# An encoder block's instruction planner: its estimates of matmul times, transfer latencies and transfer rate are set anew

## Chip, cores and metric

The kernel runs on one core of a Trainium2 chip. The metric is the device time of one execution in microseconds. Before the change it is 3083.7 us, the median of three runs (3083.41 to 3086.44).

## What is computed

One layer of an encoder for 1024 tokens of 1024 numbers, all in float32:

```python
h  = rmsnorm(x, norm1_w)
p  = h @ w_in                      # q, k, v of attention; q, k, v, z of the delta rule; decay, beta; two gates
oa = rmsnorm(softmax(q1 k1) v - lam * softmax(q2 k2) v, subln_w) * 0.8    # 8 heads
og = rmsnorm(gated_delta_rule(forward) + gated_delta_rule(backward), gdn_norm_w) * silu(z)   # 8 heads
x  = x + (sigmoid(gate_a) * (oa @ w_proj_attn) + sigmoid(gate_g) * (og @ w_proj_gdn)) @ w_out
h2 = rmsnorm(x, norm2_w)
# 16 experts; each takes the 128 tokens with the highest softmax(h2 @ w_router)
x  = x + sum_e scatter(top_e * ((silu(h2_e @ w_gate_e) * (h2_e @ w_up_e)) @ w_down_e))
out = rmsnorm(x, norm_f_w)
```

The delta rule works in chunks: in each, a triangular system is solved, and a state of 128 x 128 numbers is carried from one chunk to the next, in both directions.

## The kernel before

**Stages.** The first norm and the decay (to about 44 us); the delta rule, head after head (to 960); attention (to 1617); the two projections, the output projection with the second norm and the router, and the choice of tokens, called top-k (to about 1910); then 16 experts, and a last norm of all rows.

**How products are made.** A float32 product is made of three products of float32r parts: a high part (a rounded copy, by ScalarE) and a low part (the rest, a subtraction by VectorE or GpSimd). That pair of instructions is called a split. `mm3` issues the three matmuls, with 512 columns for dense work. Dense products read weights that are loaded in tiles of 512 KB, split and then used (class `Dense`); those of the delta rule's and attention's input, and of the gates, are the filler for TensorE while heads and rows go through dependent steps.

**Delta rule, by head** (class `Head`). `decay` loads two rows of `dG` from DRAM, each broadcast to 128 partitions, and `main` makes `U2` from them. The diagonal blocks are written to DRAM (`dl`), read back in another order as `Lu`, solved by VectorE in 15 steps, written to DRAM again (`dw`) and read back as `WN`. Three `merges` tasks then join blocks: a block transpose on VectorE (`flip`), a matmul, a copy, a matmul, a predicated copy. Two `chain` tasks carry the states of both directions; every step is a matmul that waits for VectorE or ScalarE.

**Experts** (class `Experts`). An expert has 4 units. A unit takes four parts of 1 MB of gate and up weights and two of down weights; SP loads a part into one of ten buffers, the splitter turns it into one of four pairs of high and low parts (ScalarE copies 128 x 2048 numbers, VectorE subtracts), and `worker` uses it for 12 matmuls of 512 columns. `gate` makes the activation of a unit, `prep` transposes it on TensorE (four transposes), copies the result out of PSUM (ScalarE, 128 x 512) and makes its low part, which the down product needs. The buffer of a part is free when VectorE has subtracted. At the end `tail` reads all rows back, `final_pair` applies the last norm to two tiles of them, and `last` adds what the last expert gives and scatters its rows.

**What sets the order.** No order is written down. Tasks hand their instructions to `Emit`, which holds an imagined clock for each engine and one for transfers. `run` takes, among the instructions whose inputs are issued, the one that could start first by these clocks, and by priority where two could start at once; `issue` moves the clock of the engine on by the cost that the helper (`mm`, `act`, `tt`, `dma`) gave. Each engine of the chip then works through its own instructions in just that order and waits, at each, for what it needs. The clocks are in ns. `LAT` has what passes between one engine's end and another's start; a transfer ends 650 after SP has issued it plus its length divided by a rate, and one after another.

Of the kernel before, what the change touches and what calls it, by code (L numbers as in the profile page):

```python
# [45 lines left out]
# ---------------------------------------------------------------- emission order  # L46
#
# Everything on the chip's SBUF and PSUM lies in two tiles; tags name slots in them. The work
# is cut into tasks (generators); the instructions of a task go into its queue, and run() hands
# them on one by one, in the order in which an estimate of the engines' clocks lets them start.  # L50
# [25 lines left out]
class Block:  # L76
    """A range of SBUF (or all of PSUM): one tile at a time, each of one type."""
# [27 lines left out]
class Op:  # L105
    __slots__ = ("eng", "cost", "load", "acc", "fn", "block", "ready", "prio", "kind", "dma")


class Emit:
# [15 lines left out]
    # ---- slots  # L125
# [80 lines left out]
    # ---- tasks  # L206
# [66 lines left out]
    def op(self, eng, cost, fn, writes, reads, load=0, kind="", dma=0):  # L273
        o = Op()
        o.eng, o.cost, o.fn, o.load, o.kind, o.dma = eng, cost, fn, load, kind, dma
        o.acc = [self.region(a, True) for a in writes] + [self.region(a, False) for a in reads]
        o.prio = self.cur.opprio
        q = self.cur.q
        o.block = {p for p in q if p.eng and ((eng == "pe" and p.eng == "pe") or self.conflict(p, o))}
        o.ready = None if o.block else self.when(o)  # L280
        q.append(o)

    def order(self, a, ea, b, eb):
        """Whether b must wait for a: in PSUM also for other engines' accesses to its bank."""
# [14 lines left out]
    def issue(self, t, o):  # L299
# [4 lines left out]
        if o.dma:  # L304
            who = "dma"
            end = self.dma_clk = max(end + 650, self.dma_clk) + o.dma
# [73 lines left out]
    # ---- instructions  # L380

    def mm(self, out, lhsT, rhs, start, stop):
        n = free(rhs)
        if rhs.dtype == F32R:
            c, l = (n if n >= 256 else 4 * n) / 2.4 + 2.5, 55
        else:
            c, l = max(4 * n / 2.4 + 4, 214), 109
# [54 lines left out]
    def flip(self, out, in_):  # L442
        """Every 32 x 32 block transposed in its place."""
# [19 lines left out]
    def dma(self, out, in_):  # L463
# [3 lines left out]
        self.op("sp", 478, lambda: self.nc.sync.dma_start(out, in_), [out], [in_], 0, "dma", max(n / 360.0, 112))  # L467

    def pdma(self, out, in_):
# [3 lines left out]
        self.op("pool", 1100, lambda: self.nc.gpsimd.dma_start(out, in_), [out], [in_], 0, "pdma", max(n / 360.0, 112))  # L473
# [26 lines left out]
    def prsqrt(self, y, x, t):  # L500
        """The same with the steps on GpSimd."""
# [10 lines left out]
    def rsqrt(self, y, x, t):  # L512
        """y = x^-1/2 with t as room for two tiles."""
# [14 lines left out]
# ---------------------------------------------------------------- where things lie  # L528

def plan(e):  # L530
    """Blocks, and the tags in them: name, size, number, by phase."""
# [21 lines left out]
    # first norm, decay  # L553
# [3 lines left out]
    # gated delta rule  # L557
# [6 lines left out]
    # attention  # L564
# [4 lines left out]
    # projections  # L569
# [11 lines left out]
    # experts  # L581
# [10 lines left out]
    # psum  # L592
# [9 lines left out]
# ---------------------------------------------------------------- dense products  # L602

class Dense:
    """Products with streamed weights: a loader, a splitter into two float32r parts and the
    matrix work, which fills the tensor engine whenever nothing else can run."""
# [69 lines left out]
def proj_ns(g, evac, wait=None):  # L676
    """[n, s] product of one 128-column weight tile with the first norm's output."""
# [22 lines left out]
# ---------------------------------------------------------------- first norm  # L700
# [52 lines left out]
# ---------------------------------------------------------------- decay and beta  # L753

def logit_job(g):
    """Decay and beta logits [32, s]."""
# [83 lines left out]
# ---------------------------------------------------------------- gated delta rule  # L840
# [6 lines left out]
class Head:  # L847
# [66 lines left out]
    def decay(self, dr):  # L914
# [5 lines left out]
        e.dma(d.v.rearrange("p t x -> p (t x)"), bcast(g.dG[dr * 8 + h:dr * 8 + h + 1, :], [P, S]))  # L920
# [1145 lines left out]
```

## Time and profile before

| what | value |
|---|---|
| median of three runs | 3083.7 us |
| the profiled execution, span from its first to its last instruction | 3079.2 us |
| TensorE busy, share of the span | 2883.4 us, 94% |
| VectorE | 2361.6 us, 77% |
| ScalarE | 1750.1 us, 57% |
| GpSimd | 545.7 us, 18% |
| moved by DMA | 598.52 MB |

The page gives no other time of the profiled execution than its span; the runs' median lies 4.5 us above it. Busy shares are means over stages that differ: the same engine can be the limit in one and wait in another, so a stage is read from the busy time in its own stretch, and a wait from the instruction that waited and from what stood before it in its queue. Since every engine keeps to its order, a short instruction that waits holds up all that stands behind it, needed or not.

### The profile page before, as it was taken

The page shows a single profiled execution, that of the slowest core. Times are in us where ns is not written, and L with a number is a line of the kernel's source. Part 1 is how long each engine was busy: PE and PEld are TensorE (multiplying, and loading weights), DVE is VectorE, ACT ScalarE, POOL GpSimd, SP SyncE. Part 2 cuts the span into 40 slices and gives each one's busy share as a digit, 9 for nine tenths or more (in the row PEclk, how much of TensorE's full clock was granted, in tenths as well). Part 3 has the DMA queues.
Part 4 walks back from the last instruction along what each step waited for, and adds up shares of the span by engine and source line. Part 5 has one row for each costly group of instructions (what it writes and reads, how often), then busy time and mean ns, then how long its engine had stood idle before and what let it go on. Part 6 is the DMA issues. An engine that isn't in the chain of part 4 may idle for free.

```text
span 3079.2 us, 40415 instructions
## 1 busy us (share of the span) xinstructions
PE 2883.4 (94%) x14692; PEld 2378.0 (77%) x14692; DVE 2361.6 (77%) x3837; ACT 1750.1 (57%) x2669; POOL 545.7 (18%) x457
## 2 busy tenths in 40 slices
PE   7999999999998999999999993999999999999996
PEld 6787888778787878888787772888777777777775
DVE  7768778777865777777862466998888888888887
ACT  5435444444533666676752322777767767776775
POOL 3222312222222111111225334000000000000001
PEclk9999999999999999999999996999999999999998
DMA  4222322221232111112549635999999999999996
GB/s 137 55 73 72 83 71 58 79 70 55 80 80 57 42 49 49 49 49 58 175 141 290 206 110 233 364 372 382 361 367 364 365 368 371 366 367 366 364 335 246
DMA packets 203352, 598.52 MB, mean 194 GB/s; under 512 B 84224, under 2 KB 102016, under 8 KB 154000
## 3 DMA queue, kind: packets, MB, share of 16 engines
q1 hardware_dynamic: 189568, 561.86, 50.8%
q0 software_dynamic: 13584, 34.08, 4.0%
q8 instruction: 115, 1.88, 0.2%
q14 instruction: 85, 0.70, 0.1%
HBM read 534.99 MB, written 52.49 MB: 191 GB/s over the span
## 4 chain that ended last, share of the span: by engine, by line
PE 66%; DVE 18%; ACT 4%; DMA 4%; issue 3%; SPq 1%; POOL 1%; ACTq 0%; POOLq 0%; DVEq 0%
PE psum L388 62%; DVE B L406 6%; PE psum L392 4%; DVE B L431 4%; ACT B L400 2%; DVE B L435 2%; DVE A L406 1%; SPq L467 1%; ACT A L400 1%; DVE B L425 1%; ACT psum L400 1%; DVE C L457 1%; DVE C L458 1%; DMA B<-in_w_gu_dram 1%; DMA dw<-B 1%
## 5 line engine op out<-in xcount | busy, mean ns | idle before, releaser
L388 PE MATMUL psum<-A,W 128*128 128x512 f32 (+1 forms) x5856 | 1561.2, 406 | 22.9 <-DVE A L406 14.1
L388 PEld LDWEIGHTS psum<-A,W 128*128 128x128 f32 (+1 forms) x5856 | 1062.6, 188 | 244.7 <-DVE A L406 22.0
L388 PE MATMUL psum<-B 128*128 128x128 f32 (+3 forms) x3494 | 655.6, 324 | 14.3 <-DVE B L439 7.6
L388 PEld LDWEIGHTS psum<-B 128*128 128x128 f32 x3494 | 542.4, 190 | 93.1 <-DVE B L439 11.1
L400 ACT ACTIVATE B<-psum 128x512 f32<-128x512 f32 (+4 forms) x612 | 266.2, 441 | 409.2 <-PE psum L392 230.4
L400 ACT ACTIVATE B<-B 128x2048 fp32r<-128x2048 f32 (+5 forms) x339 | 378.2, 1124 | 175.1 <-DVE B L431 80.1
L410 POOL TENSOR_TENSOR W<-W,W 128x1024 fp32r<-128x1024 f32 (+1 forms) x105 | 264.1, 2516 | 954.8 <-ACT W L400 812.8
L406 DVE TENSOR_TENSOR B<-B,B 128x2048 fp32r<-128x2048 f32 (+2 forms) x187 | 367.1, 1971 | 31.8 <-ACT B L400 25.7
L388 PE MATMUL psum<-B,W 128*128 128x512 f32 x1536 | 375.6, 397 | 1.5
L388 PEld LDWEIGHTS psum<-B,W 128*128 128x128 f32 x1536 | 285.9, 188 | 77.0 <-DVE B L406 9.9
L400 ACT ACTIVATE B<-psum,B 128x128 f32<-128x128 f32 (+2 forms) x264 | 190.9, 728 | 197.3 <-PE psum L388 124.7
L392 PE MATMUL psum<-C,B 128*128 128x128 f32 (+1 forms) x1392 | 218.4, 280 | 76.2 <-DVE B L431 27.2
L406 DVE TENSOR_TENSOR A<-B,A 128x2048 fp32r<-128x2048 f32 x115 | 261.2, 2286 | 17.7 <-ACT A L400 16.4
L388 PE MATMUL psum<-A,B 128*128 128x512 f32 x1024 | 268.6, 401 | 6.1 <-DVE A L406 3.2
L392 PEld LDWEIGHTS psum<-C,B 128*128 128x128 f32 (+1 forms) x1392 | 170.1, 143 | 128.1 <-DVE B L431 35.1
L400 ACT ACTIVATE A<-B 128x2048 fp32r<-128x2048 f32 (+1 forms) x124 | 228.6, 1858 | 44.3 <-PE psum L388 32.4
L388 PEld LDWEIGHTS psum<-A,B 128*128 128x128 f32 x1024 | 190.8, 190 | 45.2 <-DVE A L406 3.9
L388 PE MATMUL psum<-B,B 128*128 128x128 f32 (+1 forms) x1024 | 211.2, 293 | 12.2 <-DVE B L444 10.1
L481 POOL DMA_INDIRECT dx<-B,C x15 | 23.9, 1591 | 1037.5 <-ACT B L400 1037.5
L388 PEld LDWEIGHTS psum<-B,B 128*128 128x128 f32 x1024 | 174.9, 191 | 40.3 <-DVE B L444 13.9
L435 DVE TENSOR_REDUCE B<-psum 128x1 f32<-128x1024 f32 (+1 forms) x136 | 157.2, 1157 | 54.1 <-PE psum L388 52.9
L410 POOL TENSOR_TENSOR B<-B,B 128x128 f32<-128x128 f32 (+3 forms) x98 | 129.9, 1329 | 307.4 <-ACT B L400 218.8
(95 smaller groups left out, 2786.2 us busy)
## 6 DMA issues: line engine op xcount, KB each, us to landing
B<-in_w_gu_dram SPq DMA_DIRECT2D x152, 1024.0 KB, 7.1
A<-in_w_gu_dram SPq DMA_DIRECT2D x78, 1024.0 KB, 7.3
B<-in_w_dn_dram SPq DMA_DIRECT2D x77, 1024.0 KB, 6.5
A<-in_w_dn_dram SPq DMA_DIRECT2D x37, 1024.0 KB, 6.3
W<-in_w_gu_dram SPq DMA_DIRECT2D x26, 1024.0 KB, 7.2
W<-in_w_gdn_dram SPq DMA_DIRECT2D x32, 512.0 KB, 3.7
B<-dG SPq DMA_DIRECT2D x32, 512.0 KB, 5.3
W<-in_w_proj_dram SPq DMA_DIRECT2D x32, 512.0 KB, 4.5
```

What stands on the lines that cost most here:

```text
L388: self.op("pe", c, lambda: self.nc.tensor.matmul(out, lhsT, rhs, start=start, stop=stop), [out], [lhsT, rhs], l, "mm")
L392: self.op("pe", 109, lambda: self.nc.tensor.transpose(out, in_, ident), [out], [in_, ident], 55, "tr")
L400: self.op("act", c, lambda: self.nc.scalar.activation(out, in_, func, **kw), [out] + w, [in_] + r, 0, "act")
L406: self.op("dve", 69 + 1.041 * free(out), lambda: self.nc.vector.tensor_tensor(out, a, b, op), [out], [a, b], 0, "tt")
L410: self.op("pool", 150 + 2.104 * free(out), lambda: self.nc.gpsimd.tensor_tensor(out, a, b, op), [out], [a, b], 0, "ptt")
L425: lambda: (self.nc.vector.tensor_scalar(out, a, s1, None, op0=op0) if s2 is None else self.nc.vector.tensor_scalar(out, a, s1, s2, op0=op0 ...
L431: lambda: self.nc.vector.scalar_tensor_tensor(out, a, s, b, op0=op0, op1=op1),
L435: self.op("dve", 69 + 1.041 * free(in_), lambda: self.nc.vector.tensor_reduce(out, in_, axis=AX.X, op=op), [out], [in_], 0, "red")
L457: (lambda: V.match_replace(y, val, x, -1.0), [y], [val, x], "mr"),
L458: (lambda: V.max_index(idx, val, x), [idx], [val, x], "maxi")]
L467: self.op("sp", 478, lambda: self.nc.sync.dma_start(out, in_), [out], [in_], 0, "dma", max(n / 360.0, 112))
L481: self.op("pool", 1100, lambda: self.nc.gpsimd.indirect_dma_start(out=dst, out_offset=bass.IndirectOffsetOnAxis(ap=idx, axis=0), in_=y, in ...
```

## The change

In `mm`, a float32r product of n columns is reckoned at (n + 43) / 2.4 ns in place of n / 2.4 + 2.5 (below 256 columns 4n / 2.4, without the 2.5), a float32 product at 4n / 2.4 + 9, at least 222, in place of 4n / 2.4 + 4, at least 214. The rate of transfers is 380 bytes per ns in place of 360. A transfer may carry an extra latency, `slow`, which delays what reads it, but not the transfers behind it; seven calls give one. Section comments and docstrings are blanked, so line numbers move by one or two. The computation is the same.

```diff
@@ issue
             who = "dma"
-            end = self.dma_clk = max(end + 650, self.dma_clk) + o.dma
+            end = max(end + 650, self.dma_clk) + o.dma
+            self.dma_clk = end - o.slow
@@ mm
         if rhs.dtype == F32R:
-            c, l = (n if n >= 256 else 4 * n) / 2.4 + 2.5, 55
+            c, l = (n + 43 if n >= 256 else 4 * n) / 2.4, 55
         else:
-            c, l = max(4 * n / 2.4 + 4, 214), 109
+            c, l = max(4 * n / 2.4 + 9, 222), 109
@@ dma (pdma has the same rate)
-    def dma(self, out, in_):
+    def dma(self, out, in_, slow=0):
-        self.op("sp", 478, lambda: self.nc.sync.dma_start(out, in_), [out], [in_], 0, "dma", max(n / 360.0, 112))
+        self.op("sp", 478, lambda: self.nc.sync.dma_start(out, in_), [out], [in_], 0, "dma", max(n / 380.0, 112) + slow, slow)
@@ Head.decay (and qG in Head.kvprep): broadcasts of dG
-        e.dma(d.v.rearrange("p t x -> p (t x)"), bcast(g.dG[dr * 8 + h:dr * 8 + h + 1, :], [P, S]))
+        e.dma(d.v.rearrange("p t x -> p (t x)"), bcast(g.dG[dr * 8 + h:dr * 8 + h + 1, :], [P, S]), 1700)
@@ Head.main: blocks read back, solution written (both halves)
-            e.dma(Lu[64 * dr:64 * dr + 64], dl[:, :, dr, :].rearrange("r q x -> q r x"))
+            e.dma(Lu[64 * dr:64 * dr + 64], dl[:, :, dr, :].rearrange("r q x -> q r x"), 800)
-        e.dma(dw[:, :, 1, :].rearrange("r q x -> q r x"), W[0:64])
+        e.dma(dw[:, :, 1, :].rearrange("r q x -> q r x"), W[0:64], 500)
@@ proj_job: gates and the other branch's part
-        e.dma(th.v, g.dgate[1 - k, n, :, hs])
+        e.dma(th.v, g.dgate[1 - k, n, :, hs], 1100)
-            e.dma(yv.v, g.dyg[sh, n])
+            e.dma(yv.v, g.dyg[sh, n], 1100)
```

What this does to the order is shown at three places. A row is one instruction or several equal ones; L388 and L389 are the matmul of `mm`, L392 and L393 the transpose, L400 and L401 `act`.

The first is TensorE in the middle of the experts, before. `psum<-C_76,B_82` are the transposes of an activation, the 128x512 rows are products of one unit's weights, 12 to a part (`B_7778`, `A_78` and `W_111` are the blocks of memory that they read).

```order
L388 MATMUL psum<-B_7778,W_111 128x512 x24
L388 MATMUL psum<-A_78,B_7778 128x512 x17
L392 MATMUL psum<-C_76,B_82 128x128 x4
L388 MATMUL psum<-A_78,B_7778 128x512 x7
L388 MATMUL psum<-B_7778,W_111 128x512 x24
L388 MATMUL psum<-A_78,W_111 128x512 x24
L388 MATMUL psum<-B_7778 128x512 x9
L392 MATMUL psum<-C_76,B_82 128x128 x4
L388 MATMUL psum<-B_7778 128x512 x15
L388 MATMUL psum<-A_78,W_111 128x512 x24
```

And now, the same work (`B_7815` and `W_112` are the same blocks).

```order
L389 MATMUL psum<-B_7815,W_112 128x512 x24
L389 MATMUL psum<-A_78,W_112 128x512 x24
L389 MATMUL psum<-B_7815 128x512 x23
L393 MATMUL psum<-C_76,B_82 128x128 x4
L389 MATMUL psum<-B_7815 128x512
L389 MATMUL psum<-A_78,W_112 128x512 x24
L389 MATMUL psum<-B_7815,W_112 128x512 x24
L389 MATMUL psum<-A_78,B_7815 128x512 x23
L393 MATMUL psum<-C_76,B_82 128x128 x4
L389 MATMUL psum<-A_78,B_7815 128x512
```

Before, the transposes stand 17 and 9 products into a group of 24; now 23 products in, one before its end, in all units but those that also hold the transposes of the next expert's rows.

The second is ScalarE at the end of the kernel, before. `B_82<-psum` is a unit's activation function, `B_7778<-psum` the copy of its transposes, 128x2048 a split's copy, 128x1024 the last norm.

```order
L400 ACTIVATE B_82<-psum 128x512
L400 ACTIVATE B_7778,C_77<-B_13903 128x1024
L400 ACTIVATE B_13903<-B_13903,C_77 128x1024
L400 ACTIVATE B_7778<-psum 128x512
L400 ACTIVATE A_78<-W_83 128x2048
L400 ACTIVATE A_78<-B_13903 128x2048
L400 ACTIVATE B_13903<-B_13903,C_77 128x1024
L400 ACTIVATE B_7778<-B_13903 128x2048
L400 ACTIVATE B_7778<-A_13121 128x2048
L400 ACTIVATE B_7778,C_77<-B_13903 128x1024 x4
L400 ACTIVATE B_13903<-B_13903,C_77 128x1024
L400 ACTIVATE psum,C_77<-A_13121 128x1024
```

And now.

```order
L401 ACTIVATE A_78<-W_83 128x2048
L401 ACTIVATE A_78<-B_13903 128x2048
L401 ACTIVATE B_7815<-B_13903 128x2048
L401 ACTIVATE B_7815,C_77<-B_13903 128x1024
L401 ACTIVATE B_82<-psum 128x512
L401 ACTIVATE B_7815<-A_13123 128x2048
L401 ACTIVATE B_13903<-B_13903,C_77 128x1024
L401 ACTIVATE B_7815,C_77<-B_13903 128x1024 x2
L401 ACTIVATE B_7815<-psum 128x512
L401 ACTIVATE B_7815,C_77<-B_13903 128x1024
L401 ACTIVATE B_13903<-B_13903,C_77 128x1024 x2
L401 ACTIVATE psum,C_77<-A_13123 128x1024
```

Before, four splits (two pairs, `A_78` and `B_7778`) stand behind the last copy of transposes; now none does, and the norm's squares stand among the splits.

The third is TensorE where the merges of the fifth head begin, before. `psum<-B_80,B_81` is a merge's first product, `psum<-B_80` its second, `C_76,B_81` are transposes of other steps, 128x512 is filler.

```order
L388 MATMUL psum<-B_80,B_81 128x128
L388 MATMUL psum<-A_78,W_111 128x512
L388 MATMUL psum<-B_80,B_81 128x128
L388 MATMUL psum<-A_79,W_111 128x512
L388 MATMUL psum<-B_80,B_81 128x128
L388 MATMUL psum<-B_80 128x128
L392 MATMUL psum<-C_76,B_81 128x128 x2
L388 MATMUL psum<-B_80 128x128
L392 MATMUL psum<-C_76,B_81 128x128
L388 MATMUL psum<-B_80 128x128
L392 MATMUL psum<-C_76,B_81 128x128
L388 MATMUL psum<-A_78,W_111 128x512 x2
```

And now.

```order
L389 MATMUL psum<-B_80,B_81 128x128
L393 MATMUL psum<-C_76,B_81 128x128 x2
L389 MATMUL psum<-B_80,B_81 128x128
L393 MATMUL psum<-C_76,B_81 128x128
L389 MATMUL psum<-B_80,B_81 128x128
L389 MATMUL psum<-B_80 128x128
L393 MATMUL psum<-C_76,B_81 128x128
L389 MATMUL psum<-B_80 128x128
L389 MATMUL psum<-A_78,W_112 128x512
L389 MATMUL psum<-A_79,W_112 128x512
L389 MATMUL psum<-A_78,W_112 128x512 x2
L389 MATMUL psum<-A_79,W_112 128x512
```

Before, filler stood between the first products of the three merges; now transposes do, and the filler comes after the second products.

## Rows read from the trace of the kernel before

**Rows 1.** The page: span; busy us, share of the span, instructions.

```profile
span 3079.2 us, 40415 instructions
...
PE 2883.4 (94%) x14692; PEld 2378.0 (77%) x14692; DVE 2361.6 (77%) x3837; ACT 1750.1 (57%) x2669; POOL 545.7 (18%) x457
```

**Rows 2.** Stages: length; busy us of PE, PEld, DVE, ACT, POOL; clock, DMA share, GB/s.

```profile
44.00:960.00 916.00, 868.61 (x4900) 734.73 (x4899) 682.26 (x1971) 408.49 (x1148) 223.71 (x194) 0.99 0.26 70
960.00:1617.00 657.00, 624.58 (x3518) 526.18 (x3517) 492.34 (x769) 428.43 (x804) 135.28 (x62) 0.99 0.26 76
...
1985.00:2124.00 139.00, 139.00 (x627) 113.07 (x626) 125.55 (x77) 103.69 (x70) 5.25 (x4) 1.00 0.99 377
...
2195.00:2910.00 715.00, 702.24 (x3121) 562.02 (x3120) 621.26 (x381) 501.38 (x351) 24.66 (x19) 1.00 0.96 367
```

**Rows 3.** The chain that ended last: start, us, what (pieces longest).

```profile
1979.64 16.92 PE psum L388 x73
...
2049.01 16.92 PE psum L388 x73
2066.36 16.68 PE psum L388 x72
...
2188.65 18.32 PE psum L388 x79
...
2903.66 18.31 PE psum L388 x79
```

**Rows 4.** Timeline of one expert: start, us, engine, work [idle before, releaser].

```profile
2523.35 0.60 PE L392 MATMUL psum<-C,B 128*128 128x128 f32 x4
...
2523.70 3.70 PE L388 MATMUL psum<-B 128*128 128x512 f32 x15
2523.99 0.60 ACT L400 ACTIVATE B<-psum 128x512 fp32r<-128x512 f32 x1 [5.67 <-PE psum L392]
2524.48 3.71 ACT L400 ACTIVATE A<-B 128x2048 fp32r<-128x2048 f32 x2
...
2526.42 4.50 DVE L406 TENSOR_TENSOR A<-B,A 128x2048 fp32r<-128x2048 f32 x2 [1.11 <-ACT A L400]
...
2527.24 0.40 PE L388 MATMUL psum<-A,W 128*128 128x512 f32 x1
...
2528.77 5.63 PE L388 MATMUL psum<-A,W 128*128 128x512 f32 x23 [1.13 <-DVE A L406]
```

**Rows 5.** SP's waits from 2150 to 2950: total us, times, longest.

```profile
SPq L467 <- DVE B L406: 378.0, 134, 5.7
SPq L467 <- DVE A L406: 312.2, 134, 5.8
```

**Rows 6.** Timeline of the end, TensorE and the last scatter.

```profile
3039.03 0.66 PE L392 MATMUL psum<-C,B 128*128 128x128 f32 x4 [0.78 <-DVE B L406]
...
3042.56 1.22 PE L388 MATMUL psum<-A,B 128*128 128x512 f32 x2 [2.87 <-ACT A L400]
...
3046.99 7.79 PE L388 MATMUL psum<-A,B 128*128 128x512 f32 x22 [3.21 <-DVE A L406]
...
3071.36 1.00 POOL L486 DMA_INDIRECT out_dram<-A,C  x1 [8.39 <-DMA out_dram<-B]
```

**Rows 7.** Waits from 44 to 960, TensorE's and VectorE's.

```profile
PE psum L388 <- DVE B L444: 10.1, 11, 2.3
...
DVE B L444 <- DMA B<-dw: 19.1, 3, 9.6
...
DVE B L406 <- DMA B<-dl: 7.6, 3, 4.3
```

**Rows 8.** DMA from 2552.3 to 2623.8: GB/s in 40 slices, packets.

```profile
GB/s 238 435 431 435 399 371 348 380 376 225 238 401 431 433 426 422 408 435 280 399 417 412 376 307 390 293 298 110 422 408 312 376 394 426 426 426 307 316 325 348
DMA packets 3720, 26.10 MB, mean 365 GB/s; under 512 B 409, under 2 KB 409, under 8 KB 665
```

More of the change, by code (lines that the diff above doesn't have):

```diff
@@ L105 @@
 class Op:
-    __slots__ = ("eng", "cost", "load", "acc", "fn", "block", "ready", "prio", "kind", "dma")
+    __slots__ = ("eng", "cost", "load", "acc", "fn", "block", "ready", "prio", "kind", "dma", "slow")
 class Emit:
@@ L271, in conflict, with op @@
         return False
-    def op(self, eng, cost, fn, writes, reads, load=0, kind="", dma=0):
+    def op(self, eng, cost, fn, writes, reads, load=0, kind="", dma=0, slow=0):
         o = Op()
-        o.eng, o.cost, o.fn, o.load, o.kind, o.dma = eng, cost, fn, load, kind, dma
+        o.eng, o.cost, o.fn, o.load, o.kind, o.dma, o.slow = eng, cost, fn, load, kind, dma, slow
         o.acc = [self.region(a, True) for a in writes] + [self.region(a, False) for a in reads]
@@ L472, in pdma @@
             n *= x
-        self.op("pool", 1100, lambda: self.nc.gpsimd.dma_start(out, in_), [out], [in_], 0, "pdma", max(n / 360.0, 112))
+        self.op("pool", 1100, lambda: self.nc.gpsimd.dma_start(out, in_), [out], [in_], 0, "pdma", max(n / 380.0, 112))
     def gather(self, out, src, idx):
@@ L1001, in main @@
         e.cp(Wt[64:128], W[64:128].rearrange("p r x -> p x r"))
-        e.dma(dw[:, :, 1, :].rearrange("r q x -> q r x"), W[0:64])
-        e.dma(dw[:, :, 0, :].rearrange("r q x -> q r x"), Wt[64:128])
+        e.dma(dw[:, :, 1, :].rearrange("r q x -> q r x"), W[0:64], 500)
+        e.dma(dw[:, :, 0, :].rearrange("r q x -> q r x"), Wt[64:128], 500)
         e.free(sub)
@@ L1088, in kvprep @@
         for dr in range(2):
-            e.dma(qG[:, dr], bcast(g.dG[dr * 8 + h:dr * 8 + h + 1, :], [P, S]))
+            e.dma(qG[:, dr], bcast(g.dG[dr * 8 + h:dr * 8 + h + 1, :], [P, S]), 1700)
             e.act(qG[:, dr], qG[:, dr], AF.Exp)
```

## The prediction, made before the changed kernel ran

> **What bounds the kernel now.** I read the page's busy shares first, then busy time by stage, the chain of waits, the timeline of one expert, the waits of SP, and the end. The profiled execution's span is 3079.2 us and TensorE is busy for 94% of it [rows 1]; the median of the runs, 3083.7, lies 4.5 us above the span, and I carry that 4.5 over. What can still be won is therefore TensorE's own waiting, and the stages differ [rows 2]. Gated delta rule (44 to 960): busy 868.6 of 916, 47.4 idle. Attention (960 to 1617): 624.6 of 657, 32.4 idle. Early experts (1985 to 2124): 139.0 of 139, nothing idle. Later experts (2195 to 2910): 702.2 of 715.
>
> The chain shows what the later experts lose. The same place recurs at 1979.64 and 2049.01, 69.37 us apart, and from 2188.65 to 2903.66 ten times in 715.0 us, 71.50 apart [rows 3]. The work of an expert is the same 288 matmuls of 512 columns and 24 transposes, so 2.13 us an expert is lost from about the fourth on. The timeline shows where [rows 4]: TensorE's four transposes run at 2523.35; ScalarE has waited 5.67 us for them, and only after copying their result may it start the next split of weights, which stands behind that copy in its queue. The split is a ScalarE copy and a VectorE subtraction; its subtraction is needed 15 + 1 = 16 matmuls after the transposes, and TensorE waits 1.13 us for it. From the copy of the transposes to that matmul it takes 2528.77 - 2523.99 = 4.8 us, which is 4.8 / 0.2317 = 21 matmuls (16.68 us for 72, [rows 3]). With fewer than 21 matmuls between the transposes and the first product that needs the subtraction queued behind their copy, TensorE waits.
>
> Transfers are not what paces this stage: SP waits for VectorE to hand back a buffer for 378.0 + 312.2 of 800 us [rows 5].
>
> **The change, part by part.** The comments and docstrings that go issue nothing, and the new field only carries an estimate. No instruction is added or removed: the numbers change, and with them the order.
>
> *Matmul estimates.* A 512-column product was reckoned at 215.8 ns and is now 555 / 2.4 = 231.3; the trace has 231.7 [rows 3]. A transfer of 1 MB was 2913 ns and is now 2759. So the planner used to believe that 24 transfers (69.9 us), gather and scatter (2 x 1.46) bound an expert, and its products (288 x 0.2158 + 24 x 0.109 = 64.8) didn't; once its imagined stock of weights was used up, it let splits come late and put evacuation copies ahead of them. Now it has 69.1 against 69.2, a tie, and TensorE never starves in it. The order bears this out. I counted on ScalarE and TensorE, for each of the 64 copies of transposed activations, the matmuls between its transposes and the first need of the subtraction of the split queued right behind it: before, 36 to 48 for the first twelve, then 29, and from there 21, 20, 16, 28 over and over; now 38 or 40, with 47 and 30 for the last two. All of the new distances are over 21, so this wait should go in all experts. What becomes late next is TensorE itself: an expert at 69.37, as the early ones show.
> Sum for the experts, against the profiled execution: from 2049.01 to 2903.66 there are 12 periods, 854.65 - 12 x 69.37 = 22.2 us. Bounds: nothing, if another queue takes the wait over, and 22.2, since 69.37 has no TensorE idle time left in it [rows 2]. I take 22.
>
> *The end.* At 2903.66 two experts and 24 matmuls are left, 600 in all. TensorE's second but last row ends at 3046.99 + 7.79 = 3054.8 and 24 matmuls follow [rows 6], so it ends at about 3060.3: 156.6 us against 600 x 69.37 / 288 = 144.5, 12.1 lost. The core of it are waits of 0.78, 2.87 and 3.21 us at the last transposes, since four splits stand behind the last copy on ScalarE. In the new order all four stand ahead of it, and the first final-norm operations have moved up beside the last gate products. A dependent hop stays there: transposes 0.66, a copy of 0.60 [rows 4] and a subtraction of such a size, of which the four matmuls that are left between cover 0.9; with final-norm work in VectorE's queue I leave 3 of the 12 us standing. Gain 9; bounds -2 (the final norm's reads, issued earlier, hold up ScalarE's queue by more than today) and 12. The 19 us behind TensorE's end I leave as they are: the last scatter waits for the output's writes either way, 8.39 us today [rows 6].
>
> *Longer latencies for the broadcasts of decay, for the solve's two rewrites and for gate reads; and what the matmul numbers do before 1617.* VectorE waits 19.1 us for the solve's result and 7.6 for its input to come back from DRAM [rows 7]; work that the planner now puts ahead of these waits can hide them. At best all 26.7 us return, and only where TensorE waited with it. Against that stands the second effect of the matmul numbers: the too-short estimates made the planner put more filler products between dependent steps than it thought, a margin of 231.7 / 215.8, 7%. Now there is less: counted in the order over all heads, filler between the 511 pairs of merge instructions that follow each other falls from 1.28 to 1.04 products a pair, about 126 products, while chains gain some 25. In the worst case each of the 126 returns as waiting, 126 x 0.2317 = 29 us; waits at merges cost 10.1 / 11 = 0.9 us apiece today [rows 7]. Filler is not lost, it runs elsewhere, under other waits. Between -27 and +29 I take 0: TensorE's waiting in that stage, 47.4 of 916 [rows 2], is small against the work that both effects only move about.
>
> *Rate of the POOL loads and small changes in projections, router and top-k.* The rates set when a load is thought to land, not when it does; in these stages the order moves by a few products and top-k's chain on VectorE is the same. Nothing, within 3 us; without that cover it is a wait or two of rival 2's price.
>
> Sum: -22 - 9 + 0 = -31 us, span 3048, median 3052.
>
> **A page against this.** Over an expert of the steady stretch 26.10 MB move in 71.5 us, 365 GB/s [rows 8]; at 69.37 it must be 376. Stretches of under 2 us in that same expert reach 420 to 435 [rows 8], and the early experts held 377 for 139 us with TensorE full [rows 2]. The Trainium skill, "DMA: Bandwidth & Descriptors", section "Where 436 GB/s comes from", has the HBM side bind transfers to SBUF at about 358 GB/s. By that rule an expert could not take less than 26.10 / 358 = 72.9 us (an estimate from that page's figure) and the change would win nothing there. The rows above are already over it, and the measurement decides.
>
> **Rivals.**
> 1. *Transfers pace the experts after all.* If 367 GB/s, the mean of 2195 to 2910 [rows 2], were the most that can be had for long, an expert stays at 26.10 / 0.367 = 71.1 us: ten experts win 0.4 each, the end at most 5. For it: the DMA share is 0.96 there. Against it: SP waits for buffers, not for transfers to land, and 377 was held. About 3075. With the page's figure the experts would win nothing and the end alone would be left: about 3079, an estimate.
> 2. *The early stages pay for the margin (slower).* Place: merges and chains of the delta rule and the rows of attention, where TensorE now comes to a dependent product just when the estimate has it ready, and VectorE is late. Price: 0.9 us a wait. It decides from 31 us, some 34 new waits, on; that is today's 79.8 us of idle time (47.4 + 32.4) growing by two fifths. With 45 us, 3098. For it: filler between merges does fall. Against it: transposes take over part of the cover, and the latencies are now nearer to the chip.
> 3. *The early stages gain too.* Half of the 26.7 us that VectorE waits for DRAM, with TensorE's waits behind it: 3052 - 14 = 3038.
>
> **How the numbers follow.** Forecast (experts -22, end -9, the rest within 12 either way) 0.76, own range 3040 to 3066; rival 3 0.11; rival 1 0.07; rival 2 0.06. The range of 8 in 10 takes in half of rival 3 and ends before rival 1: 3035 to 3070. A measurement of this kernel tells about 0.2%, 6.2 us, from no change: faster is under 3077.5, slower over 3089.9. Forecast and rival 3 are faster, rival 1 about half: 0.89. Same 0.06, slower 0.05.
>
> **What would show it.** Right: experts 69.4 us apart from the second to the fifteenth, TensorE without idle time between 1985 and 2910, ScalarE's waits for transposes short there, and under 4 us of TensorE waits in the last 48 matmuls. Wrong: a period that stays at 71.5 with SP no longer waiting for buffers (rival 1) or with a new engine named ahead of the products; the place that recurs, at 1979.64 before, first coming more than 15 us later, with more TensorE idle time before 1617 (rival 2). The experts are the step I am surest of; the 0 for the early stages is the weakest.

## The result: slower by 0.8%, and the profile after

The changed kernel takes 3107.0 us (median of four runs, 3104.4 to 3108.0) against 3083.6 for the kernel before: ratio 1.0078, 95% interval 1.0064 to 1.0092. 3052 was forecast. The profiled execution spans 3105.7 us, 26.5 more than before [rows 1]:

```profile
span 3105.7 us, 40409 instructions
...
PE 2894.6 (93%) x14692; PEld 2390.7 (77%) x14692; DVE 2377.3 (77%) x3837; ACT 1771.1 (57%) x2669; POOL 560.4 (18%) x457
```

Two large differences hide in the 26.5. The first matmul of the first expert starts at 1973.2 us, before at 1913.7: 59.5 lost. From there to the last matmul it takes 1112.5 us, before 1146.2: 33.7 won. Behind the last matmul nothing changed (19 to 20 us in both). Busy time by stage, as in [rows 2]:

```profile
44.00:990.00 946.00, 887.58 (x4959) 747.43 (x4957) 693.79 (x1977) 410.78 (x1158) 218.84 (x195) 0.99 0.25 68
990.00:1665.00 675.00, 626.08 (x3460) 521.99 (x3461) 489.61 (x762) 424.63 (x797) 132.82 (x58) 0.97 0.24 72
2044.00:2183.00 139.00, 139.00 (x626) 113.02 (x626) 125.13 (x77) 103.88 (x70) 8.80 (x4) 1.00 0.99 375
2252.00:2960.00 708.00, 708.00 (x3184) 575.76 (x3183) 637.71 (x388) 529.49 (x358) 41.19 (x20) 1.00 0.99 377
```

The experts are what was forecast: no TensorE idle time in 708 us, and no wait of ScalarE for transposes over 1.0 us, before 5.67 [rows 4]. The chain, as in [rows 3], has the recurring place every 69.4 us, twelve periods in 832.87:

```profile
2107.83 16.94 PE psum L389 x73
...
2177.22 16.93 PE psum L389 x73
...
2940.70 16.92 PE psum L389 x73
```

The end answers to [rows 6]: TensorE's waits there are 0.19 and 1.62 us, the scatter's 7.60.

```profile
3076.46 0.60 PE L393 MATMUL psum<-C,B 128*128 128x128 f32 x4
...
3078.40 1.20 PE L389 MATMUL psum<-B 128*128 128x512 f32 x4 [0.19 <-ACT B L401]
3081.22 4.83 PE L389 MATMUL psum<-B 128*128 128x512 f32 x20 [1.62 <-DVE B L407]
...
3097.86 1.00 POOL L488 DMA_INDIRECT out_dram<-A,C  x1 [7.60 <-DVE A L432]
```

The loss is spread over the stages ahead. Two stretches that together hold the same TensorE work in each kernel (to the first transposes of attention's first values, and on to the first of the last 384 projection products), before and then after:

```profile
43.00:1003.00 960.00, 903.10 (x5051) 762.09 (x5050) 711.76 (x2012) 424.88 (x1185) 235.97 (x198) 0.99 0.26 70
1003.00:1651.50 648.50, 625.60 (x3523) 527.36 (x3522) 467.67 (x735) 420.39 (x777) 143.67 (x76) 1.00 0.30 88
```

```profile
46.00:1012.00 966.00, 900.21 (x5001) 757.44 (x5001) 709.62 (x2010) 417.38 (x1179) 218.84 (x195) 0.98 0.26 70
1012.00:1704.50 692.50, 650.95 (x3572) 541.79 (x3571) 479.27 (x737) 426.39 (x783) 156.90 (x79) 0.98 0.28 82
```

Idle time grows from 56.9 + 22.9 = 79.8 us to 65.8 + 41.5 = 107.3, by 27.5. TensorE's busy time grows by 22.5 as well, for the same work. The granted clock falls to its lower level (1.2 for 2.4 GHz) more often: 64.9 us at half clock over both stretches, before 23.9. The sums over just these pieces, before and then after, show how much of them was work:

```profile
sum 23.90, PE 20.24 PEld 17.28 DVE 18.05 ACT 8.71 POOL 6.78; mean PE 3.37 PEld 2.88 DVE 3.01 ACT 1.45 POOL 1.13
sum 64.85, PE 50.58 PEld 42.67 DVE 36.67 ACT 19.05 POOL 5.26; mean PE 4.21 PEld 3.56 DVE 3.06 ACT 1.59 POOL 0.44
```

30.3 us more of busy time at half speed are 15.2 us of work; where the other 7 come from is not shown. The rest of the 59.5 is 3 before 46 us and 6.5 behind 1704.5.

One head change of attention shows both halves of the loss. Timeline of the changed kernel:

```profile
1241.27 6.92 POOL L411 TENSOR_TENSOR B<-B,B 64x1024 fp32r<-64x1024 f32 x2 [7.02 <-ACT B L401]
1242.47 2.25 DVE L432 SCALAR_TENSOR_TENSOR B<-B 128x8 f32<-128x8 f32 x1
...
1246.01 2.20 DVE L432 SCALAR_TENSOR_TENSOR B<-B 128x8 f32<-128x8 f32 x1
...
1248.44 0.37 DVE L432 SCALAR_TENSOR_TENSOR B<-B 128x8 f32<-128x8 f32 x2
1248.85 1.23 DVE L407 TENSOR_TENSOR C<-C,B 128x1024 f32<-128x1024 f32 x1
1250.22 1.09 PE L393 MATMUL psum<-C,C 128*128 128x128 f32 x4 [5.69 <-DVE C L407]
1250.96 1.63 PE L389 MATMUL psum<-A,W 128*128 128x512 f32 x3
```

VectorE normalizes a finished head by small steps; two of them last 2.2 us beside GpSimd's two passes over 64 x 1024 numbers, the two at 1248.44 take 0.19 us each. The transposes that need the result stand in TensorE's queue ahead of dense products, and TensorE waits 5.69 us. During that wait the clock falls, and stays low for 6.8 us (the column third from the end):

```profile
1244.60:1247.50 2.90, 0.00 (x0) 0.00 (x0) 2.84 (x3) 0.45 (x1) 2.83 (x2) 1.00 0.00 0
1247.50:1254.30 6.80, 4.08 (x13) 3.33 (x14) 2.86 (x6) 1.29 (x3) 0.68 (x1) 0.50 0.12 39
1254.30:1261.00 6.70, 6.70 (x36) 5.57 (x36) 3.69 (x2) 3.68 (x8) 2.39 (x1) 0.99 0.12 39
```

### The profile page after: what moved, and what is told of

Its sections match the earlier page's. It is cut to its first block, busy times and chain, and to the rows that moved or that the text cites. A ratio compares the mean times of both kernels' runs of the same rounds, so it can differ in the third digit from the quotient of the medians.

```text
span 3105.7 us, 40409 instructions
## 1 busy us (share of the span) xinstructions
PE 2894.6 (93%) x14692; PEld 2390.7 (77%) x14692; DVE 2377.3 (77%) x3837; ACT 1771.1 (57%) x2669; POOL 560.4 (18%) x457
## 4 chain that ended last, share of the span: by engine, by line
PE 68%; DVE 19%; ACT 5%; DMA 4%; issue 2%; SPq 1%; POOL 1%; POOLq 0%; DVEq 0%; ACTq 0%
PE psum L389 63%; DVE B L432 6%; DVE B L407 6%; PE psum L393 4%; ACT B L401 3%; DVE B L436 2%; SPq L469 1%; DVE B L426 1%; DMA B<-in_w_out_dram 1%; DVE C L458 1%; ACT psum L401 1%; DVE C L459 1%; DMA B<-B 1%; DVE B L440 1%; POOL B L411 1%
## 5 line engine op out<-in xcount | busy, mean ns | idle before, releaser
L389 PE MATMUL psum<-A,W 128*128 128x512 f32 (+1 forms) x5856 | 1552.0, 406 | 4.6 <-POOL W L411 3.0
L389 PEld LDWEIGHTS psum<-A,W 128*128 128x128 f32 (+1 forms) x5856 | 1073.9, 189 | 225.0 <-POOL W L411 5.7
L389 PE MATMUL psum<-B 128*128 128x128 f32 (+3 forms) x3494 | 666.5, 327 | 26.6 <-DVE B L440 13.1
L389 PEld LDWEIGHTS psum<-B 128*128 128x128 f32 x3494 | 540.5, 191 | 114.2 <-DVE B L440 16.4
L401 ACT ACTIVATE B<-B 128x2048 fp32r<-128x2048 f32 (+6 forms) x339 | 380.5, 1126 | 218.6 <-DVE B L432 83.7
L401 ACT ACTIVATE B<-psum 128x512 f32<-128x512 f32 (+4 forms) x612 | 266.3, 441 | 328.3 <-PE psum L389 173.8
L407 DVE TENSOR_TENSOR B<-B,B 128x2048 fp32r<-128x2048 f32 (+2 forms) x187 | 370.4, 1981 | 63.1 <-ACT B L401 52.9
L389 PE MATMUL psum<-B,W 128*128 128x512 f32 x1536 | 368.8, 395 | 0.0
L389 PEld LDWEIGHTS psum<-B,W 128*128 128x128 f32 x1536 | 288.5, 188 | 69.3
L393 PE MATMUL psum<-C,B 128*128 128x128 f32 (+1 forms) x1392 | 221.9, 284 | 95.5 <-DVE B L432 31.4
L401 ACT ACTIVATE B<-psum,B 128x128 f32<-128x128 f32 (+2 forms) x264 | 190.7, 727 | 176.5 <-PE psum L389 111.9
L393 PEld LDWEIGHTS psum<-C,B 128*128 128x128 f32 (+1 forms) x1392 | 172.1, 145 | 146.0 <-DVE B L432 41.2
L401 ACT ACTIVATE A<-B 128x2048 fp32r<-128x2048 f32 (+1 forms) x124 | 231.1, 1864 | 78.9 <-PE psum L389 55.7
L389 PE MATMUL psum<-A,B 128*128 128x512 f32 x1024 | 269.9, 400 | 0.0
L389 PE MATMUL psum<-B,B 128*128 128x128 f32 (+1 forms) x1024 | 211.7, 294 | 15.6 <-DVE B L445 13.6
L389 PEld LDWEIGHTS psum<-A,B 128*128 128x128 f32 x1024 | 189.4, 189 | 36.9
L389 PEld LDWEIGHTS psum<-B,B 128*128 128x128 f32 x1024 | 173.3, 192 | 44.3 <-DVE B L445 13.7
L436 DVE TENSOR_REDUCE B<-psum 128x1 f32<-128x1024 f32 (+1 forms) x136 | 156.8, 1155 | 46.8 <-PE psum L389 43.6
```

The source lines that it names most:

```text
L389: self.op("pe", c, lambda: self.nc.tensor.matmul(out, lhsT, rhs, start=start, stop=stop), [out], [lhsT, rhs], l, "mm")
L393: self.op("pe", 109, lambda: self.nc.tensor.transpose(out, in_, ident), [out], [in_, ident], 55, "tr")
L401: self.op("act", c, lambda: self.nc.scalar.activation(out, in_, func, **kw), [out] + w, [in_] + r, 0, "act")
L407: self.op("dve", 69 + 1.041 * free(out), lambda: self.nc.vector.tensor_tensor(out, a, b, op), [out], [a, b], 0, "tt")
L436: self.op("dve", 69 + 1.041 * free(in_), lambda: self.nc.vector.tensor_reduce(out, in_, axis=AX.X, op=op), [out], [in_], 0, "red")
```

## The experiments

Three theories stood against each other: the margin that the too-short matmul numbers gave (the prediction's second rival), the new latencies, and a mere reshuffle of the order. For each kernel the table has the start of the first expert's first matmul; TensorE time lost in three stretches (start of a matmul less the full-clock time of all matmuls ahead of it, so idle time and half clock together): up to the first transposes of attention's first values, from there to attention's last matmul, and in the output projection with the router; the period of the eleventh expert (from its first matmul to the twelfth's); and the time (a median of 4 to 10 runs for the changed kernel, the three parts alone and the two kernels with new matmul numbers in the experts only; a single run for the others; before itself took 3079 to 3084 beside them). "Old" and "new" are the matmul numbers that planned the early stages.

| kernel | first expert | lost: start | attention | router | expert | us |
|---|---|---|---|---|---|---|
| before (old) | 1913.7 | 109.5 | 32.0 | 6.9 | 71.5 | 3083.6 |
| rate alone (old) | 1927.8 | 119.1 | 38.5 | 6.9 | 70.9 | 3084.2 |
| float32r +2 ns (old) | 1945.3 | 124.0 | 47.9 | 8.2 | 71.5 | 3112.6 |
| fp32 +2 ns (old) | 1937.5 | 114.0 | 50.0 | 7.9 | 71.5 | 3104.9 |
| transpose +2 ns (old) | 1925.6 | 120.9 | 33.5 | 7.8 | 71.5 | 3093.6 |
| latencies alone (old) | 1962.3 | 133.6 | 58.4 | 7.0 | 71.5 | 3129.3 |
| latencies, fp32 +2 ns (old) | 1924.2 | 111.4 | 40.6 | 8.0 | 71.5 | 3091.7 |
| after (new) | 1973.2 | 129.7 | 64.7 | 12.2 | 69.4 | 3107.0 |
| after, float32r +2 ns (new) | 1979.5 | 134.1 | 66.2 | 12.4 | 69.4 | 3115.6 |
| after, fp32 +2 ns (new) | 2002.4 | 144.3 | 80.4 | 12.1 | 69.4 | 3137.6 |
| after, transpose +2 ns (new) | 1983.4 | 132.0 | 66.8 | 12.1 | 69.4 | 3117.3 |
| matmul numbers alone (new) | 1989.4 | 145.8 | 64.3 | 12.1 | 71.1 | 3146.8 |
| new from attention on | 1950.1 | 107.4 | 61.8 | 12.2 | 69.4 | 3085.0 |
| new up to attention | 1977.2 | 151.6 | 55.1 | 7.1 | 69.4 | 3111.4 |
| after, stretched 1.26 / 1.12 | 1939.5 | 135.3 | 34.4 | 4.6 | 69.3 | 3073.8 |
| after, stretched 1.20 / 1.10 | 1961.9 | 133.2 | 47.7 | 7.5 | 69.3 | 3096.7 |
| after, stretched from the start | 2008.8 | 156.8 | 79.8 | 4.7 | 69.4 | 3145.6 |
| matmul numbers, experts only | 1913.1 | 109.1 | 31.5 | 7.1 | 71.1 | 3069.9 |
| rate 440, experts only (old) | 1913.5 | 109.5 | 31.7 | 7.0 | 69.4 | 3045.5 |
| numbers and rate, experts only | 1914.0 | 108.9 | 31.4 | 7.0 | 69.4 | 3045.4 |

**One part at a time.** In the kernel before: the two new lines of `mm` alone, the `slow` arguments alone, the rate alone.

```diff
e1  -c, l = (n if n >= 256 else 4 * n) / 2.4 + 2.5, 55     -c, l = max(4 * n / 2.4 + 4, 214), 109
    +c, l = (n + 43 if n >= 256 else 4 * n) / 2.4, 55      +c, l = max(4 * n / 2.4 + 9, 222), 109
e2  -max(n / 360.0, 112))                                  +max(n / 360.0, 112) + slow, slow)
e3  -max(n / 360.0, 112))                                  +max(n / 380.0, 112))
```

> The kernel before with the new matmul estimates alone; latencies and rate stay as they were. Margin theory (the too-short matmul estimates gave slack between dependent steps, and the exact ones use it up): it carries nearly the whole loss, first expert matmul at 1960 to 1980 us (before 1913.7, after 1973.2), experts at 69.4 us each, 3095 to 3110 us in all. Latency theory (the estimates of transfers moved the early stages): first expert matmul at 1910 to 1925, 3045 to 3060 in all. Reshuffle theory (any change of an estimate throws the order of the stages before the experts, with no sign of its own): the first expert matmul lies more than 8 us from both 1913.7 and 1973.2.

> The longer latencies alone; matmul estimates and rate as before. Margin theory: within 8 us of before, 3076 to 3092 us, first expert matmul within 8 us of 1913.7, experts at 71.5 us. Latency theory: first expert matmul at 1950 to 1975, 3115 to 3145 in all. Reshuffle theory: first expert matmul more than 8 us from 1913.7, to either side.

> The transfer rate of 380 for 360 alone. Margin theory and latency theory: within 8 us of before, 3076 to 3092 us, first expert matmul within 8 us of 1913.7. Reshuffle theory: although no matmul and no latency is changed, the first expert matmul is more than 8 us from 1913.7, to either side.

Ratios 1.0224 (1.0207 to 1.0241), 1.0166 (1.0149 to 1.0183) and 1.0011 (1.0001 to 1.0020). Only the reshuffle theory had all three right: each part alone moves the first expert by more than 8 us, and the three shifts (75.7, 48.6 and 14.1) don't add up to the 59.5 of the whole. The matmul numbers alone are even worse than the changed kernel; with them the experts run at 69.4 us from the second to the seventh and at 71.1 from the ninth on, with the rate alone at 69.4 up to the fifth and at 70.9 from the seventh on.

**How much is luck.** One estimate moved by 2 ns in the kernel before, and the same three in the changed one:

```diff
p1  -... / 2.4 + 2.5, 55                      +... / 2.4 + 4.5, 55
p2  -max(4 * n / 2.4 + 4, 214), 109           +max(4 * n / 2.4 + 6, 216), 109
p3  -self.op("pe", 109, lambda: ...transpose  +self.op("pe", 111, lambda: ...transpose
a1  -(n + 43 if n >= 256 ...                  +(n + 48 if n >= 256 ...
a2  -max(4 * n / 2.4 + 9, 222), 109           +max(4 * n / 2.4 + 11, 224), 109
a3  as p3
```

> The kernel before with one estimate moved by next to nothing: a float32r matmul counts 2 ns more (217.8 for 215.8 ns at 512 columns), a tenth of the change's own step. Margin theory: at most a tenth of the change's effect, the first expert matmul within 6 us of 1913.7. Reshuffle theory: the plan's order changes all the same, and the first expert matmul lies more than 8 us off; if before was a lucky order among many, later.

> The kernel before with an fp32 matmul counted 2 ns longer (216 for 214 ns at 128 columns), a quarter of the change's own step of 8. Margin theory: at most a quarter of the change's effect, the first expert matmul 0 to 15 us after 1913.7, never before it. Reshuffle theory: off by more than 8 us, to either side; later, if before was a lucky order.

> The kernel before with a transpose on TensorE counted 2 ns longer (111 for 109 ns), which is not part of the change. Margin and latency theories: within 6 us of 1913.7. Reshuffle theory: off by more than 8 us, to either side; later, if before was a lucky order.

> The changed kernel with a float32r matmul counted 2 ns longer (233.3 for 231.25 ns). Theory of luck alone (the new numbers are no worse in the early stages than the old ones; before was a lucky order, the changed kernel an unlucky one): three such small steps scatter about the mean of the four neighbours of before, first expert matmul at 1934 on average, 1915 to 1955 each. Theory that the new numbers also cost something of their own: 1955 to 1995, about the changed kernel's 1973. Experts at 69.4 us by both.

> The changed kernel with an fp32 matmul counted 2 ns longer (224 for 222 ns). Luck alone: first expert matmul at 1915 to 1955 us; a cost of the new numbers' own: 1955 to 1995.

> The changed kernel with a transpose on TensorE counted 2 ns longer (111 for 109 ns). Luck alone: first expert matmul at 1915 to 1955 us; a cost of the new numbers' own: 1955 to 1995.

Next to nothing costs the kernel before 12 to 32 us. With the rate alone, its four neighbours have the first expert at 1934 on average, so the order of before is a lucky one, by some 20 us. The changed kernel and its neighbours lie at 1973 to 2002 (one of them above the 1995 expected at most), 1985 on average, with no overlap: some 50 us are the new numbers' own, matmul, latencies and rate together. The 59.5 of the changed kernel are these 50 and the 20 by which before was lucky, less some 11 by which the changed kernel comes ahead of its own average. Both averages are over four draws of one profiled execution each, which scatter by 20 to 30 us; the runs of before itself spread from 3076.6 to 3086.4.

**The latencies** alone looked as bad as the matmul numbers. A neighbour of that run, with the fp32 line of p2 above, tells otherwise:

> The longer latencies alone, with an fp32 matmul counted 2 ns longer: a neighbour of the run with the latencies alone, whose first expert matmul was at 1962. If the latencies cost in themselves: 1950 or later again. If that order was only unlucky: 1920 to 1946, as the neighbours of before.

1924.2, below all four neighbours of before: the 1962 was an unlucky order, and a cost of the latencies' own is not shown.

**What in the matmul numbers does it.** In the router a row's softmax is planned to be short, and really lasts about 4.5 us. TensorE of before, from the row's logits (128x16) to the transposes of its softmax; the row ahead of the transposes closes 14 dense matmuls:

```profile
1772.90 1.85 PE L388 MATMUL psum<-B,A 128*128 128x16 f32 x16
...
1777.67 0.39 PE L388 MATMUL psum<-B,B 128*128 128x512 f32 x1
1779.22 0.27 PE L392 MATMUL psum<-C,B 128*16 128x128 f32 x1 [1.16 <-DVE B L425]
```

In the changed kernel 12 stand there, and the wait is longer:

```profile
1827.83 1.85 PE L389 MATMUL psum<-B,A 128*128 128x16 f32 x16
1829.53 0.70 PE L389 MATMUL psum<-A,B 128*128 128x512 f32 x2
1830.08 0.63 PE L389 MATMUL psum<-B,B 128*128 128x512 f32 x2
1830.55 1.08 PE L389 MATMUL psum<-A,B 128*128 128x512 f32 x4
1831.47 0.62 PE L389 MATMUL psum<-B,B 128*128 128x512 f32 x2
1831.93 0.61 PE L389 MATMUL psum<-A,B 128*128 128x512 f32 x2
1834.37 0.27 PE L393 MATMUL psum<-C,B 128*16 128x128 f32 x1 [1.83 <-DVE B L426]
```

14 x 215.8 ns and 12 x 231.25 ns are 3.0 and 2.8 us in the plan: it fills the same imagined gap with as many products as it believes to fit. VectorE's last step is what it underrates (timeline of before):

```profile
1776.68 2.37 POOL L410 TENSOR_TENSOR A<-A 128x1024 f32<-128x1024 f32 x1 [1.26 <-ACT A L400]
...
1776.98 0.16 DVE L451 RECIPROCAL B<-B 128x1 f32<-128x1 f32 x1 [1.37 <-ACT B L400]
1777.17 1.90 DVE L425 TENSOR_SCALAR B<-B 128x16 f32<-128x16 f32 x1
```

Planned at 0.14 us, it takes 1.90 and ends 0.02 us after GpSimd's pass. That agrees with the Trainium skill, "SBUF — State Buffer", section "SBUF: two separate sides", where VectorE and GpSimd share a pair of ports that one of them locks for a whole instruction. Over the attention of before, VectorE's instructions (its copies left out) are planned at 347.0 us and last 435.7, 1.26 times; 42.0 of the 88.7 more lie in the 82 that run mostly beside GpSimd. ScalarE's are planned at 373.0 and last 419.3, 1.12 times. These are sums of instruction times, which overlap a little: by ScalarE's busy time there, 404.7 us, it is 1.085 times. So the old matmul numbers, 7% short, stood beside others that were shorter still. The test leaves the new matmul numbers and stretches the others:

```diff
-        o.eng, o.cost, ... = eng, cost, ...
+        o.eng, o.cost, ... = eng, cost * ({"dve": 1.26, "act": 1.12}.get(eng, 1.0) if self.stage == 1 else 1.0), ...
```

> The changed kernel with the planned times of VectorE and ScalarE stretched by 1.26 and 1.12 from the point at which the last head of the gated delta rule is in the plan to the end of the top-k: by as much as their measured instruction times exceed the planned ones in the attention of the kernel before (435.7 for 347.0 us, 419.3 for 373.0). Ratio theory (the old matmul numbers were too short by about as much as those of the other engines, and the plan lives on the ratio; setting one engine right alone breaks it): TensorE loses at most 48 us in the attention (after 64.7, before 32.0, neighbours of before 33 to 50), about 1.2 us at each row of the router (after 1.8), first expert matmul at 1940 to 1958. Rival (right matmul numbers cost in themselves, or leave less cover in any case): 60 us or more in the attention, first expert matmul at 1968 or later.

> The same with 1.20 and 1.10, a second draw of the order. Ratio theory: at most 50 us lost in the attention, first expert matmul at 1940 to 1960. Rival: 60 us or more, 1968 or later.

The row at this place is back to 14 matmuls and less waiting than before:

```profile
1813.45 1.85 PE L389 MATMUL psum<-B,A 128*128 128x16 f32 x16
...
1818.00 0.61 PE L389 MATMUL psum<-B,B 128*128 128x512 f32 x2
1819.55 0.27 PE L393 MATMUL psum<-C,B 128*16 128x128 f32 x1 [0.94 <-DVE B L426]
```

And the attention stage, stretched by 1.26 and 1.12, against the changed kernel's:

```profile
1025.00:1627.00 602.00, 581.30 (x3319) 490.87 (x3318) 453.29 (x708) 406.72 (x756) 114.08 (x52) 0.99 0.25 72
```

```profile
1012.00:1636.00 624.00, 584.18 (x3281) 488.39 (x3280) 462.62 (x708) 409.87 (x760) 121.10 (x50) 0.97 0.22 63
```

Idle 20.7 for 39.8 us, half clock 6.8 for 34.1. Lost in all 34.4 and 47.7 for 64.7, and in the router 4.6 and 7.5 for 12.2: in these two draws attention and router live on the ratio between the engines' numbers. The second draw's first expert comes 2 us later than expected, with 14.5 us lost between attention and output projection (after 7.6).

**Stage by stage.** The new numbers from the last head of the delta rule on (g3), then the same the other way round (g4):

> The kernel before up to the last head of the gated delta rule, then the new matmul numbers, and the new rate from the end of the top-k on. If the new matmul numbers cost in the attention by themselves: TensorE is at the first transposes of the attention's first values within 3 us of before (1002.6) and then loses 55 us or more in the attention (before 32.0) and 12 us in the output projection with the router (before 7.0): first expert matmul at 1938 to 1952, 3069 to 3083 us in all. If the attention loses by the state in which the stage before leaves it: 32 to 50 us lost there, 1913 to 1932, 3044 to 3063.

> The new matmul numbers up to the last head of the gated delta rule, the old ones through attention, output projection and router, the new ones with the new rate from the end of the top-k on: the other half of the run with the new numbers in the later stages. If the numbers cost in both stages separately: 130 us or more lost at the first transposes of the attention's values (before 109.5), then 32 to 50 us in the attention and 7 in the output projection with the router; first expert matmul at 1935 to 1960. If the attention loses by the state in which the stage before leaves it: 58 us or more lost in it.

```diff
-            c, l = (n if n >= 256 else 4 * n) / 2.4 + 2.5, 55
+            c, l = ((n + 43 if n >= 256 else 4 * n) / 2.4 if self.stage else ... / 2.4 + 2.5), 55      # g3; g4: if self.stage != 1
```

`stage` is 0 up to the last head of the delta rule, 1 from there, 2 from the end of the top-k on. The later stages pay by themselves: 61.8 and 12.2 us after a start like that of before. In all the kernels with old numbers in attention it loses 31 to 58, with new ones unstretched 62 to 80, a narrow gap; the router 6.9 to 8.2 and 12.1 to 12.4. The counterpart loses 151.6 ahead of attention, but its 55.1 in attention lie between the two expectations, and its first expert, at 1977.2, behind the 1960 that separate costs allowed: whether a part of that comes from the stage before stays open.

**The delta rule.** The same stretch, from the first instruction on (1.25 and 1.12 while `stage` is under 2).

> The changed kernel with VectorE's and ScalarE's planned times stretched by 1.25 and 1.12 from the first instruction on, to the end of the top-k. In its own plan TensorE now loses 83 us up to the last head's merges, where the changed kernel's plan has 18. Ratio theory for the gated delta rule too: TensorE has lost at most 122 us at the first transposes of the attention's values (after 129.7, neighbours of before 111 to 124), first expert matmul at 1950 or earlier. Rival (there the loss comes from the dense matmuls that fill in: a plan that sees the waits spends them sooner and has none left at the end of the stage): 135 us or more lost by then, with more than 15 of them between the last head's merges and the end of its chain (after 6.4), first expert matmul at 1955 or later.

The rival's signs came (156.8 us lost by then, first expert at 2008.8), those of the ratio theory did not; but the five heads ahead of the loss speak for the ratio. Columns as above, stretched from the start, to the sixth head's merges and from there to attention; then the changed kernel to the sixth head's merges:

```profile
44.00:715.00 671.00, 657.73 (x3614) 553.71 (x3615) 498.87 (x1393) 298.68 (x817) 175.06 (x151) 1.00 0.27 76
715.00:1072.00 357.00, 298.47 (x1554) 245.20 (x1553) 225.18 (x629) 135.88 (x377) 70.31 (x50) 0.89 0.18 46
```

```profile
44.00:716.00 672.00, 628.91 (x3433) 526.90 (x3432) 496.64 (x1391) 290.12 (x805) 157.67 (x145) 0.99 0.26 71
```

For five heads the ratio does it: 13.3 us idle in place of 43.1. But TensorE does 181 matmuls more in that row, dense products that fill in, and in the last three heads they run short: 58.5 us idle in 357 at a mean clock of 0.89. The cover is a stock: what is spent early is missing late. Attention, stretched as above, has fewer products left too, 3211 matmuls for the 3319 of the kernel stretched by 1.26 and 1.12, and loses 79.8 us:

```profile
1072.00:1695.00 623.00, 573.00 (x3211) 485.09 (x3209) 434.87 (x702) 398.11 (x748) 110.24 (x49) 0.96 0.23 68
```

So the ratio alone does not save attention when the filler is short; the router keeps its gain (4.7). Of the 20 us that the changed kernel loses ahead of attention beyond before, no run tells apart what is ratio, what is stock and what is luck.

**The experts.** Three kernels with the early stages of before; `fit` is set at the end of the top-k. The first has the new matmul numbers from there on, the second the rate of 380 as well, the third a rate of 440 with the old matmul numbers.

> The new matmul estimates from the end of the top-k on alone; everything ahead of it is planned as before. All theories: first expert matmul within 2 us of 1913.7, experts at 69.4 us each from the second on and 15 of them some 25 us shorter, the end 8 to 10 us shorter: 3046 to 3056 us. If the gain of the experts needs the earlier start of the rest, or the other rate, it is smaller: 3060 to 3075.

> The new matmul estimates and the new rate, both from the end of the top-k on, all ahead of it planned as before. Theory that the experts' gain needs the planned time of the matmuls (288 x 231.25 ns = 66.6 us an expert) to be longer than the planned time of its weights (25.17 MB at 380 = 66.2 us; at 360 it is 69.9): experts at 69.4 us each to the last, the last one 70.6 for 79.8 us, 3083.6 - 34 = 3044 to 3054 us. Theory that it needs the other order of the early stages: as with the matmul numbers alone, 71.1 us from expert 7 on and 3065 to 3073.

> From the end of the top-k on a rate of 440 that the transfers do not have, with the old matmul estimates. Theory that only the comparison of the two planned times counts (weights at 440: 57.2 us an expert, matmuls as before 288 x 215.8 ns = 62.2): the plan loads ahead, and the experts run at 69.4 us to the last although no number fits the trace; 3045 to 3058 us. Theory that the numbers must fit the trace: the plan's orders come too early for the transfers, stalls as before or worse: 71 us or more from some expert on, 3070 to 3100.

```diff
-... "dma", max(n / 360.0, 112))
+... "dma", max(n / (440.0 if self.fit else 360.0), 112))
```

3069.9 (ratio 0.9969, 0.9956 to 0.9981), 3045.4 (0.9879, 0.9862 to 0.9895) and 3045.5 us. In all four combinations of matmul numbers and rate (with the two parts alone above) it is which of the two planned times is longer that counts, weights or products: a rate of 440 with the old numbers, neither of which fits the trace, runs as the right pair does. Seventy us of its experts:

```profile
2550.00:2620.00 70.00, 70.00 (x317) 56.93 (x316) 63.31 (x40) 51.80 (x35) 2.60 (x2) 1.00 1.00 383
```

The second beats both kernels: by its ratio 1.2%, 37 us, under before, and so by the two ratios 61 under the changed one.

## Why the prediction was wrong

- *Experts, -22.* Right in size and cause: twelve periods take 832.9 us where 854.7 were, 21.8 less. The tie of weights and products that the prediction worked out is the mechanism, and ScalarE's long waits for transposes are gone, as it said; either half of the change alone leaves 70.9 or 71.1. Rival 1 is out: 377 GB/s over 708 us, and 383 in the last rows.
- *End, -9.* Right: experts 15 and 16 take 11.0 us less, with 1.8 us of waits left where 3 were left standing.
- *Early stages, 0 between -27 and +29.* This step failed, and its bound with it: +52.9, 20.2 up to attention's first values and 32.7 in attention. "TensorE's waiting in that stage ... is small against the work that both effects only move about" took the waiting of before as typical. It was a draw better than its neighbours by 20 us, and any new number draws again. The bound counted the 126 products that fewer stand between merges, but the same loss of cover sits in attention, where the largest part arose (64.7 for 32.0). There the runs show in its place that right matmul numbers beside too short ones for VectorE and ScalarE leave less cover at the waits: with those stretched, attention is back at 34.4 and 47.7. For the 20.2 ahead of it the cause stays open between ratio, stock and luck. The bound also priced waits alone; some 15 us more went into work at half clock.
- *Projections, router and top-k, within 3.* Wrong: 6.6, of which the router has 5.3 (12.2 for 6.9).
- *Rival 2* named the mechanism, the place and the sign: TensorE comes when the estimate has a result ready, and VectorE is late. At a chance of 0.06 it was far underrated. Its argument against itself, latencies nearer to the chip, carried nothing that a run shows.

## What to carry to other kernels

A planner can live on the ratios of its numbers: correcting one engine's while the others stay short takes away cover that nobody put there on purpose, so correct the engines of a stage together, or, what paid most here, only the stage that is to gain. Before a change of plan is judged, move an estimate by next to nothing a few times: the scatter of such neighbours (here up to 32 us for an edit of 2 ns) is what a gain has to beat, and a kernel that was kept because it was fast may be a lucky draw. Ask, too, how much filler there is: a plan that hides early waits better can pay for it at the end of the stage.

## What the hardware showed that was not expected

A VectorE instruction on 128 x 16 numbers took 1.9 us beside a GpSimd pass, and ended with it; one of the same kind and size with GpSimd idle (at 1906.63 us of before) took 0.18. TensorE's clock fell to 1.2 GHz within a wait of 5.7 us and stayed there for 6.8 us, of which more than half was work; in attention there were 34.1 us of half clock where before had 3.4. One core's transfers held 377 GB/s for 708 us.
